# Hybrid LRU / attention / state-space backbone on one core: the state-space core starts by group and takes its steps at wider intervals

## The chip, the core and the metric

The kernel runs on one core of a Trainium2 chip, in one launch. The metric is the device time of that launch in microseconds, a median over runs. The engines are named as in the profile: PE is TensorE's matmul stream, PEld its weight loads, DVE is VectorE, ACT is ScalarE, POOL is GpSimd, SP is SyncE, which issues the transfers.

## What is computed

Two layers of a hybrid backbone over 256 context and 256 latent tokens of width 2048, in float32. Cut to what matters here:

```python
for l in range(2):
    shift, scale, gate = split(silu(cond) @ ada_w + ada_b)        # for the latents and for the context
    u = rmsnorm(x) * (1 + scale) + shift
    lx, lg, q, k, v, ag, xbc, z, dt = split_cols(u @ w_in)
    lru = rglru_mixer(lx)                                         # scan in both directions
    att = window_attention(q, k, v)                               # 8 heads, softmax over window, context and a sink
    ssd = ssd_mixer(xbc, z, dt)                                   # the state-space core, both directions
    x = x + gate * (concat(lru*silu(lg), att*silu(ag), ssd) @ w_out)

def ssd_chunked(x, dt, A, B, C, h0):                              # chunks of 128 tokens, 2 groups of 8 heads
    decay = exp(segment sums of dt * A);  W = (C . B) * decay * dt
    y_diag = W @ x                                                # inside a chunk
    states = B^T @ (x * exp(A_last - Acs) * dt);  h = exp(A_last) * h + states
    y_off = (C @ h) * exp(Acs)                                    # from the chunks before
```

`ssd_mixer` runs this twice, forwards and on the flipped sequence, and adds both. It needs xs, B and C (parts of xbc after a convolution and a silu) and dt. A group of 8 heads needs its own column of B and of C, its own four columns of xs, and dt.

## The kernel before

Weights are stored as blocks of 128x128. Every weight is split into hi (rounded to the matmul's fast float32 form, on ACT, L237) and lo (the rest, on DVE, L238), as is every activation u; a block then takes three matmuls, `hi*uh`, `hi*ul`, `lo*uh` (`mm3`, L174 is the matmul of the helper `mm`). One hi and one lo instruction serve four blocks, and there are three buffers of each (`HB`). A **tile of columns** is 128 columns of w_in: 16 blocks, 48 matmuls, of 512 token columns or, in layer 1 for what only latents need, of 256.

A layer first runs through the columns of w_in: first B, C and the first of x side by side (`HEAD`), in layer 0 with four more x between them (`FILL`), then the rest of x, then lx and lg by turns (8 each), then 8 z, 2 k, 2 v, and q and ag by turns (8 each: one attention head for every pair). Then comes w_out in three parts (`OUT_PARTS`): the LRU's eight rows, the state-space's, the attention's; 16 accumulators a part, each of 8 blocks.

What follows from a finished tile runs as a generator (`consume`): it emits instructions, yields a wait, and emits the next ones. A wait is a number of us of a modelled clock, which `mm` moves on for every matmul emitted (`WAIT`, one number per layer), or a condition. `pump` runs what is due between two blocks of the stream; `drain(until)` is called where the stream can't go on: it moves the clock to the next due time and runs the waiting generators in the order of those times until the condition holds. PE's order is the order in which the program emits; the other engines' orders come from a scheduler that places their instructions by its own estimate. All queues are in order: on PE a matmul that waits holds up all behind it.

- `ssd_core` (L612) waits until the 13 inputs (2 B, 2 C, 8 x, dt) are there. Then, for each of two groups, it makes steps: `State` (L1105: a product with Xtok on DVE, a matmul, a decayed sum on DVE) and `Output` (L1131: two decay rows by DMA, then eight DVE and eight ACT instructions over 128x128, exponentials, POOL products, and 8 to 24 small matmuls). Layer 0 has 28 steps (12 states, 16 outputs), layer 1 has 20 (12 and 8). A step's `begin` is emitted, then the core waits `WAIT["core"]` (4 us in layer 0, 5.2 in layer 1), then the step before gets its `end`, which holds its matmuls.
- `ada_wide` (L361) forms the modulation vectors that the start of a layer doesn't need, from ada_w by rows, on DVE (L380): 64 steps a part, one DMA of 256 KB into one of three buffers each. Layer 0 runs parts 0 to 2 of it after its core (that is, layer 0's gate and layer 1's shift and scale). Layer 1 runs the last one, layer 1's gate: from the head of the layer on (`ada1`, every 2.75 us), it stops when the core may begin, and goes on after the core (`ada`, every 5.97 us).
- The attention of a head (`att_q`, L802) emits scores, softmax (DVE maxima, ACT exponentials, POOL scaling, L864), then after a wait (`q2`, for the last head `q2z`: 12.98 us in layer 1) the transposes of the probabilities (L170), their split (ACT L875, DVE L877), and the product with v.
- Before the first block of w_out the layer calls `drain` until the gate vector is there:

```python
            self.drain(lambda: part in self.parts_done)
            if pi == 0:
                self.drain(lambda: self.ada_done >= (4 if l else 1))
```

The residual update of x (L1073) multiplies each accumulator of w_out by that gate; there are three accumulators (`acc`).

Of the kernel before, what the change touches and what calls it, by code (L numbers as in the profile page):

```python
# [18 lines left out]
C = 256  # L19
# [94 lines left out]
for _tag, _bufs, _roles in [  # L114
# [13 lines left out]
    for _r in _roles:  # L128
# [2 lines left out]

HB = 3
WAIT = {"B": (36.48, 14.89), "C": (28.19, 0.27), "x": (33.09, 10.71), "dt": (16.92, 0.59), "softplus":
        (19.41, 30.37), "acs": (0.94, 0.68), "core": (4, 5.2), "ada": (2.38, 5.97), "ada1": (1.17, 2.75), "z":
# [5 lines left out]
class Kernel:  # L140
# [220 lines left out]
    def ada_wide(self, parts):  # L361


        nc = self.nc
        for w in parts:
            l, part = (0, 2) if w == 0 else (1, w - 1)
            conds = 1 if w == 3 else 2
            if w < 3:
                yield lambda: self.core_done
            sums = self.t([P, conds, KT, 4], "wst" if w < 3 else "adas", 1)  # L370
            for q in range(4):
                row = [self.t([P, 4, P], "adac") for _ in range(conds)]
                for c in range(conds):
                    nc.sync.dma_start(out=row[c], in_=self.condD[4 * q:4 * q + 4, c].partition_broadcast(P))
                for m in range(KT):
                    raw = self.t([P, 512], "araw", 3)
                    nc.sync.dma_start(out=raw, in_=self.a["adaw"][w, q, m])
                    for c in range(conds):
                        o = raw if c == conds - 1 else self.ada_acc()
                        i = nc.vector.scalar_tensor_tensor(out=o, in0=raw, scalar=1.0,  # L380
                                                           in1=row[c].rearrange("p t x -> p (t x)"), op0=ALU.mult,
                                                           op1=ALU.mult, accum_out=sums[:, c, m, q:q + 1])
                        self.tc.keep_in_program_order(i)
                    yield self.wait("ada" if self.core_done else "ada1")
                    if self.ssd_ready == 13 and not self.core_done:
                        yield lambda: self.core_done
            mod = self.mods[l][:, KT * part:KT * part + KT]
            o = PARAMS["ada_b"][0] + KT * part
            for c in range(conds):
                nc.vector.tensor_reduce(out=mod[:, :, c], in_=sums[:, c], axis=AX.X, op=ALU.add)  # L390
                nc.vector.tensor_tensor(out=mod[:, :, c], in0=mod[:, :, c], in1=self.prms[l][:, o:o + KT], op=ALU.add)
            self.ada_done += 1
# [105 lines left out]
    def ssd_in(self, l, kind, i, px, t0):  # L498
        nc = self.nc
        if kind == "B":  # L500
            self.ssd_conv(8 + i, px, self.BT[:, i], 0)
            yield self.wait("B")
            self.tok_major(self.BT[:, i], self.Btok[:, :, i * P:(i + 1) * P])
        elif kind == "C":
            self.ssd_conv(10 + i, px, self.CT[:, i, t0:], t0)
            yield self.wait("C")
        else:
            xs = self.t([P, 512], "xs")
            self.ssd_conv(i, px, xs, 0)
            s = C if l else 0  # L510
            nc.gpsimd.tensor_scalar(out=self.Y[:, i, s:], in0=xs[:, s:], scalar1=self.par("Drep", i), scalar2=1.0,  # L511
                                    op0=ALU.mult, op1=ALU.mult)
            yield self.wait("x")
            self.tok_major(xs, self.Xtok[:, :, i * P:(i + 1) * P])
        self.ssd_ready += 1

    def dt_weights(self, l):
        nc = self.nc
# [26 lines left out]
    def ssd_dt2(self, dts):  # L545
# [7 lines left out]
        z = self.t([P, 2, 4, 16], "dtz", 1)  # L553
# [32 lines left out]
        self.acsD = self.dram([P, P], "acsD")  # L586
        nc.sync.dma_start(out=self.acsD, in_=at)
        yield self.wait("acs")
        self.ssd_ready += 1

    def softplus(self, z, n, tag):

# [19 lines left out]
    def ssd_core(self, l):  # L612


        yield lambda: self.ssd_ready == 13
        ends = []
        for g in range(2):
            f1, r1 = self.ssd_state(0, g, 0), self.ssd_state(1, g, 1)
            steps = [f1, r1]
            if l == 0:  # L620
# [325 lines left out]
    def layer(self, l, xs):  # L946
        nc = self.nc
        self.l = l
        mod = self.mods[l]
        self.ssd_ready = self.kv_ready = 0  # L950
        self.core_done = False
        self.lru_h, self.att_o, self.parts_done, self.mixes = {}, {}, set(), {}
        t0 = lambda kind: 0 if l == 0 or kind in CTX_COLS else C
        wst = self.blocks(self.a["w_in"][l], NW)
# [35 lines left out]
        for ct, ks in head_plan(l):  # L990
            fill = ct in FILL[l]
            acc = self.mx() if fill else accs[ct][:, cols(ct)]
            for k in ks:
# [16 lines left out]
                if k == 6 and wds is None:  # L1010
                    wds = self.dt_weights(l)
                    if l == 0:
                        i = nc.sync.dma_start(out=self.cst[:, P:], in_=self.a["consts"][:, P:])
# [43 lines left out]
        for pi, part in enumerate(OUT_PARTS):  # L1057
# [3 lines left out]
            for m in range(KT):  # L1061
# [7 lines left out]
                x = xs[m // 8][:, m % 8]  # L1069
# [205 lines left out]
```

## Time and profile before

| | |
|---|---|
| median of 3 runs | 1846.21 us (1844.5 to 1850.26) |
| the profiled execution | 1850.27 us, its span 1848.5 us |
| PE, DVE, ACT, POOL busy | 1777.5, 1424.8, 959.7, 334.9 us |
| mean granted clock of TensorE | 0.988 of full speed |
| chain that ended last | PE 74%, DVE 12%, ACT 7%, issue 4%, DMA 3% |

The span is what the profiler saw between the first and the last instruction. An engine is busy while an instruction of it runs; matmuls overlap, so a busy PE can still lose time between two starts. The arrow of a row names who ended the idle time ahead of an instruction.

### The profile page before, as it was taken

The page shows a single profiled execution, that of the slowest core. Times are in us where ns is not written, and L with a number is a line of the kernel's source. Part 1 is how long each engine was busy: PE and PEld are TensorE (multiplying, and loading weights), DVE is VectorE, ACT ScalarE, POOL GpSimd, SP SyncE. Part 2 cuts the span into 40 slices and gives each one's busy share as a digit, 9 for nine tenths or more (in the row PEclk, how much of TensorE's full clock was granted, in tenths as well). Part 3 has the DMA queues.
Part 4 walks back from the last instruction along what each step waited for, and adds up shares of the span by engine and source line. Part 5 has one row for each costly group of instructions (what it writes and reads, how often), then busy time and mean ns, then how long its engine had stood idle before and what let it go on. Part 6 is the DMA issues. An engine that isn't in the chain of part 4 may idle for free.

```text
span 1848.5 us, 29534 instructions
## 1 busy us (share of the span) xinstructions
PE 1777.5 (96%) x10522; PEld 1456.0 (79%) x10522; DVE 1424.8 (77%) x3053; ACT 959.7 (52%) x1766; POOL 334.9 (18%) x271
## 2 busy tenths in 40 slices
PE   7999999999999999999999999999999999999999
PEld 4777876666778877887878887878666788999999
DVE  4447769899998888989999547776778885788765
ACT  4324577777433354555232335544687763677543
POOL 0000124434210022221000020010243330122000
PEclk9999999999999999999999999999999999999999
DMA  9982433435775645557777443464343564555656
GB/s 377 365 295 69 124 97 106 129 111 157 220 219 175 192 145 174 172 166 245 231 221 221 129 126 107 142 183 150 96 136 109 160 202 152 174 174 165 210 184 183
DMA packets 140261, 323.09 MB, mean 175 GB/s; under 512 B 14000, under 2 KB 39504, under 8 KB 139472
## 3 DMA queue, kind: packets, MB, share of 16 engines
q1 hardware_dynamic: 140112, 321.20, 55.6%
q8 instruction: 82, 1.34, 0.3%
q14 instruction: 67, 0.55, 0.1%
HBM read 310.51 MB, written 10.63 MB: 174 GB/s over the span
## 4 chain that ended last, share of the span: by engine, by line
PE 74%; DVE 12%; ACT 7%; issue 4%; DMA 3%; POOL 1%; SPq 0%; POOLq 0%; DVEq 0%; ACTq 0%
PE acc L174 57%; PE mx L174 12%; DVE lo L238 3%; PE ada L174 3%; PE mx L170 2%; DVE ee L1161 1%; DVE ada L380 1%; ACT lt L712 1%; DVE araw L380 1%; ACT hi L237 1%; DMA bc<-acsD 1%; ACT ww L1163 1%; DMA araw<-in_adaw_dram 1%; DVE lh L730 1%; ACT ee L1160 1%
## 5 line engine op out<-in xcount | busy, mean ns | idle before, releaser
L174 PE MATMUL acc<-u,hi 128*128 128x512 f32 (+1 forms) x4800 | 1284.7, 356 | 10.7 <-ACT hi L237 6.2
L174 PEld LDWEIGHTS acc<-u,hi 128*128 128x128 f32 x4800 | 840.6, 191 | 158.3 <-issue 29.0
L174 PE MATMUL acc<-u,lo 128*128 128x512 f32 (+1 forms) x2400 | 848.8, 354 | 24.8 <-DVE lo L238 24.2
L237 ACT ACTIVATE hi<-raw 128x512 fp32r<-128x512 f32 x640 | 399.3, 629 | 588.4 <-PE acc L174 459.2
L238 DVE TENSOR_TENSOR lo<-raw,hi 128x512 fp32r<-128x512 f32 x640 | 470.1, 737 | 195.7 <-ACT hi L237 186.0
L174 PEld LDWEIGHTS acc<-u,lo 128*128 128x128 f32 x2400 | 458.0, 191 | 98.9 <-DVE lo L238 39.0
L380 DVE SCALAR_TENSOR_TENSOR araw<-araw,adac 128x512 f32<-128x512 f32 x256 | 189.5, 741 | 8.6 <-DMA araw<-in_adaw_dram 5.3
L380 DVE SCALAR_TENSOR_TENSOR ada<-araw,adac 128x512 f32<-128x512 f32 x192 | 143.1, 745 | 11.2 <-DMA araw<-in_adaw_dram 6.6
L174 PE MATMUL mx<-u,hi 128*128 128x512 f32 (+1 forms) x320 | 98.8, 392 | 0.0
L1073 DVE SCALAR_TENSOR_TENSOR X<-acc,mod,X 128x256 f32<-128x256 f32 x144 | 65.0, 478 | 38.2 <-PE acc L174 38.0
L864 POOL TENSOR_SCALAR prob<-prob,qrs 128x512 f32<-128x512 f32 (+1 forms) x48 | 58.3, 1228 | 200.0 <-ACT hi L237 158.0
L427 POOL TENSOR_TENSOR ssq<-ssq,sq 128x512 f32<-128x512 f32 (+1 forms) x26 | 32.7, 1257 | 303.2 <-ACT sq L423 303.2
L1172 POOL TENSOR_TENSOR bc<-bc,CT 128x512 f32<-128x512 f32 x40 | 62.2, 1566 | 88.2 <-ACT bc L1171 49.1
L511 POOL TENSOR_SCALAR X<-xs,prm 128x512 f32<-128x512 f32 (+1 forms) x16 | 15.4, 963 | 344.5 <-DVE xs L489 340.6
L174 PEld LDWEIGHTS mx<-u,hi 128*128 128x128 f32 x320 | 55.9, 188 | 14.1 <-issue 4.0
L720 POOL TENSOR_TENSOR la<-lt 128x512 f32<-128x512 f32 x32 | 39.0, 1221 | 134.5 <-ACT lt L718 117.1
L174 PE MATMUL mx<-u,lo 128*128 128x512 f32 (+1 forms) x160 | 60.7, 379 | 0.0
L1161 DVE SCALAR_TENSOR_TENSOR ee<-bc,nacs,ee 128x128 f32<-128x128 f32 x96 | 44.2, 509 | 18.7 <-DMA bc<-acsD 14.3
L767 POOL TENSOR_TENSOR qw<-qw,cst 128x256 f32<-128x256 f32 x20 | 22.5, 1127 | 195.2 <-DVE rt L766 131.5
L727 POOL TENSOR_TENSOR lt<-lt,ltl 128x512 f32<-128x512 f32 x32 | 47.8, 1515 | 48.4 <-ACT ltl L724 45.5
L712 ACT ACTIVATE lt<-mx,gbh 128x512 f32<-128x512 f32 x64 | 42.4, 674 | 10.0 <-PE mx L174 10.0
L174 PE MATMUL mx<-xc,gw 64*64 64x512 f32 x128 | 39.9, 615 | 4.6 <-DVE H L1128 2.2
(236 smaller groups left out, 1979.0 us busy)
## 6 DMA issues: line engine op xcount, KB each, us to landing
raw<-in_w_in_dram SPq DMA_DIRECT2D x224, 512.0 KB, 3.7
araw<-in_adaw_dram SPq DMA_DIRECT2D x256, 256.0 KB, 3.2
raw<-in_w_out_dram SPq DMA_DIRECT2D x96, 512.0 KB, 3.8
ar<-in_ada_dram SPq DMA_DIRECT2D x84, 256.0 KB, 5.9
bc<-acsD SPq DMA_DIRECT2D x48, 256.0 KB, 4.1
ar<-in_ada_dram SPq DMA_DIRECT2D x22, 512.0 KB, 7.4
adac<-condD SPq DMA_DIRECT2D x28, 256.0 KB, 4.6
gw<-in_gates_dram SPq DMA_DIRECT2D x16, 256.0 KB, 2.9
```

The source lines that it names most:

```text
L170: self.nc.tensor.transpose(out=out, in_=lhsT, identity=rhs)
L174: self.nc.tensor.matmul(out=out, lhsT=lhsT, rhs=rhs, start=start, stop=stop, **kw)
L237: nc.scalar.activation(out=hi, in_=part, func=AF.Copy)
L238: nc.vector.tensor_tensor(out=lo, in0=part, in1=hi.bitcast(F32), op=ALU.subtract)
L380: i = nc.vector.scalar_tensor_tensor(out=o, in0=raw, scalar=1.0, in1=row[c].rearrange("p t x -> p (t x)"), op0=ALU.mult, op1=ALU.mult, acc ...
L712: nc.scalar.activation(out=t, in_=pg[g], func=AF.Tanh, scale=0.5, bias=self.gb[:, 16 * g + 8 * d + m:16 * g + 8 * d + m + 1])
L720: nc.gpsimd.tensor_tensor(out=a2, in0=tr, in1=tr, op=ALU.mult)
L727: nc.gpsimd.tensor_tensor(out=ti, in0=ti, in1=tl[:, d], op=ALU.mult)
L864: nc.gpsimd.tensor_scalar(out=pr[j], in0=pr[j], scalar1=rs[:, j:j + 1], scalar2=1.0, op0=ALU.mult, op1=ALU.mult)
L1073: nc.vector.scalar_tensor_tensor(out=x[:, s], in0=acc[:, s.start - w0:s.stop - w0], scalar=mod[:, 2 * KT + m, c:c + 1], in1=x[:, s], op0=A ...
L1161: nc.vector.scalar_tensor_tensor(out=e[:, j], in0=bcs[1][:, j], scalar=k.nacs[:, r:r + 1], in1=e[:, j], op0=ALU.add, op1=ALU.min)
L1172: nc.gpsimd.tensor_tensor(out=bc, in0=bc, in1=k.CT[:, g, None, tok].to_broadcast([P, 4, P]), op=ALU.mult)
```

## The change

The count of inputs becomes a set; each group waits for its own seven inputs (B, C, four x, dt) instead of all 13; the waits between steps go from 4 and 5.2 us of the modelled clock to 5.4 and 7.6; `ada_wide` of layer 1 stops when the core has begun.

```diff
-        (19.41, 30.37), "acs": (0.94, 0.68), "core": (4, 5.2), "ada": (2.38, 5.97), "ada1": (1.17, 2.75), "z":
+        (19.41, 30.37), "acs": (0.94, 0.68), "core": (5.4, 7.6), "ada": (2.38, 5.97), "ada1": (1.17, 2.75), "z":
@@ ada_wide
                     yield self.wait("ada" if self.core_done else "ada1")
-                    if self.ssd_ready == 13 and not self.core_done:
+                    if self.core_begun and not self.core_done:
                         yield lambda: self.core_done
@@ ssd_in
-        self.ssd_ready += 1
+        self.ssd_ready.add((kind, i))
@@ ssd_dt2
-        self.ssd_ready += 1
+        self.ssd_ready.add(("dt", 0))
@@ ssd_core
-        yield lambda: self.ssd_ready == 13
         ends = []
         for g in range(2):
+            need = {("B", g), ("C", g), ("dt", 0)} | {("x", 4 * g + i) for i in range(4)}
+            yield lambda: need <= self.ssd_ready
+            self.core_begun = True
             f1, r1 = self.ssd_state(0, g, 0), self.ssd_state(1, g, 1)
@@ layer
-        self.ssd_ready = self.kv_ready = 0
-        self.core_done = False
+        self.ssd_ready, self.kv_ready = set(), 0
+        self.core_begun = self.core_done = False
```

No instruction of PE is added or removed; 8788 rows of its order stand in other places. Counted in tiles of 48 matmuls of the stream, from the first matmul with weights: in layer 0 the core's first matmul moves from tile 15.62 to 13.75 and its last group from 26.38 to 27.62 (z begins at 28); in layer 1 from 94.56 to 90.50 and from 106.81 to 107.81 (z begins at 108). So 28 steps stand on 13.9 tiles instead of 10.8, and 20 on 17.3 instead of 12.3.

**PE, layer 0, the first state of the core** (`xw` is Xtok weighted, `Btok` and `CT`, `BT` are B and C; `acc` rows are the stream, u by hi and lo). Before:

```order
L174 MATMUL acc_2595<-u_1072,hi_2634 128x512
L174 MATMUL acc_2595<-u_1073,hi_2634 128x512
L174 MATMUL acc_2595<-u_1072,lo_2635 128x512
L174 MATMUL mx_2644<-xw_2567,Btok_1769 128x512
L174 MATMUL mx_2648<-CT_1768,BT_1767 128x128
L174 MATMUL acc_2595<-u_1287,hi_2634 128x512
```

With the change:

```order
L174 MATMUL acc_2388<-u_1299,hi_2427 128x512
L174 MATMUL acc_2388<-u_1298,lo_2428 128x512
L174 MATMUL mx_2443<-xw_2351,Btok_1769 128x512
L174 MATMUL mx_2447<-CT_1768,BT_1767 128x128
L170 MATMUL mx_2479<-cst_76,xs_2151 128x128 x4
L174 MATMUL acc_2388<-u_1501,hi_2485 128x512
```

The state now stands ahead of the transposes of x's last tiles (`xs`), two tiles of the stream earlier.

**PE, layer 1, the last head's probabilities** (`prob`; `vh`, `vl` are v, `ptlh`, `ptll` the split probabilities). Before, amid w_out, whose matmuls stand on both sides:

```order
L174 MATMUL acc_17124<-u_16801,hi_17127 128x256
L174 MATMUL acc_17124<-u_16802,hi_17127 128x256
L174 MATMUL acc_17124<-u_16801,lo_17128 128x256
L170 MATMUL mx_17134<-cst_76,prob_16931 128x128 x4
L174 MATMUL acc_17124<-u_16810,hi_17127 128x256
L174 MATMUL acc_17124<-u_16811,hi_17127 128x256
```

With the change, behind the product of head 6 (`mx_16925`) and ahead of the whole of w_out:

```order
L174 MATMUL mx_16925<-ptlh_16634,vh_14693 128x256
L174 MATMUL mx_16925<-ptll_16636,vh_14693 128x256
L174 MATMUL mx_16925<-ptlh_16634,vl_14694 128x256
L170 MATMUL mx_16948<-cst_76,prob_16893 128x128 x4
L170 MATMUL mx_16956<-cst_76,prob_16895 128x128 x4
L174 MATMUL mx_16967<-ptlh_16899,vh_14693 128x256
L174 MATMUL mx_16967<-ptll_16900,vh_14693 128x256
```

Between the last scores of head 7 and these transposes now stand 4 transposes, 6 stream matmuls and the 12 of head 6's product; before there stood over 100 stream matmuls. The first w_out matmul follows the 12 of head 7's product.

**DVE, layer 1, the end of `ada_wide`** (`araw` a row of ada_w, `adas` its sums, `mod` the modulation vectors, X the residual). Before, the last steps stand amid the q tiles:

```order
L238 TENSOR_TENSOR lo_16589<-raw_16555,hi_16588 128x512
L380 SCALAR_TENSOR_TENSOR araw_16601,adas_11169<-araw_16601,adac_15138 128x512
L238 TENSOR_TENSOR lo_16610<-raw_16607,hi_16609 128x512
L390 TENSOR_REDUCE mod_33_146<-adas_11169 128x16
L766 TENSOR_TENSOR rt_3493_16579<-qw_16550,cst_76 64x256 x2
L391 TENSOR_TENSOR mod_33_146<-mod_33_146,prm_991 128x16
```

With the change they stand behind head 7's split, right ahead of the first residual updates:

```order
L380 SCALAR_TENSOR_TENSOR araw_17002,adas_11169<-araw_17002,adac_16500 128x512
L238 TENSOR_TENSOR lo_17141<-raw_17122,hi_17140 128x512
L380 SCALAR_TENSOR_TENSOR araw_17005,adas_11169<-araw_17005,adac_16500 128x512
L238 TENSOR_TENSOR lo_17161<-raw_17158,hi_17160 128x512
L380 SCALAR_TENSOR_TENSOR araw_17008,adas_11169<-araw_17008,adac_16500 128x512
L390 TENSOR_REDUCE mod_33_146<-adas_11169 128x16
L391 TENSOR_TENSOR mod_33_146<-mod_33_146,prm_991 128x16
L1075 SCALAR_TENSOR_TENSOR X_16921<-acc_17013,mod_33_146,X_16921 128x256
```

Before the core, layer 1 now has 19 of its 64 `ada_wide` steps in place of 32. Ten of them stand behind head 7's split, with six lo rows among them.

## Rows read from the trace of the kernel before

**Rows 1.** Cores of both layers: length; busy PE, PEld, DVE, ACT, POOL; clock; DMA share, GB/s.

```profile
255.00:455.00 200.00, 183.14 (x996) 128.72 (x995) 178.88 (x324) 149.04 (x296) 81.41 (x56) 0.99 0.40 114
1315.00:1465.00 150.00, 137.54 (x823) 101.93 (x822) 122.33 (x209) 111.93 (x201) 57.07 (x45) 0.97 0.41 124
```

**Rows 2.** PE's groups of instructions in layer 0's core, 255 to 455 us.

```profile
L174 PE MATMUL acc<-u,hi 128*128 128x512 f32 x360 | 118.5, 410 | 1.7 <-ACT hi L237 1.7
L174 PE MATMUL acc<-u,lo 128*128 128x512 f32 x180 | 71.5, 397 | 10.7 <-DVE lo L238 10.7
L174 PE MATMUL mx<-bc,H 128*64 128x128 f32 x192 | 19.0, 273 | 0.0
L174 PE MATMUL mx<-ee,X 128*64 128x128 f32 x128 | 18.0, 288 | 0.1
L174 PE MATMUL mx<-xc,gw 64*64 64x512 f32 x48 | 16.3, 614 | 4.3 <-DVE H L1128 2.2 <-ACT lt L712 2.0
L174 PE MATMUL mx<-xw,Btok 128*128 128x512 f32 x24 | 13.0, 626 | 0.0
```

**Rows 3.** Undisturbed pace, from the chain: start us, us, matmuls of 512 and 256 columns.

```profile
249.02 9.57 PE acc L174 x42
...
1722.67 122.06 PE acc L174 x1017
```

**Rows 4.** PE's timeline in layer 0's core: a state, gates, an output.

```profile
258.43 1.02 PE L174 MATMUL mx<-xw,Btok 128*128 128x512 f32 x2
259.28 0.38 PE L174 MATMUL mx<-CT,BT 128*128 128x128 f32 x2
...
265.25 0.65 PE L174 MATMUL mx<-xc,gw 64*64 64x512 f32 x2
...
266.27 0.73 PE L174 MATMUL acc<-u,hi 128*128 128x512 f32 x2
...
271.32 0.45 PE L174 MATMUL mx<-ee,X 128*64 128x128 f32 x4
...
272.39 0.49 PE L174 MATMUL mx<-CT,BT 128*128 128x128 f32 x2
```

**Rows 5.** DVE's groups in layer 0's core, 255 to 455 us.

```profile
L238 DVE TENSOR_TENSOR lo<-raw,hi 128x512 fp32r<-128x512 f32 x46 | 38.1, 831 | 4.3 <-ACT hi L237 4.3
L1161 DVE SCALAR_TENSOR_TENSOR ee<-bc,nacs,ee 128x128 f32<-128x128 f32 x56 | 30.6, 593 | 5.5 <-ACT ee L1160 3.0 <-DMA bc<-acsD 2.5
L1164 DVE SCALAR_TENSOR_TENSOR ww<-cbm,dt,ww 128x128 f32<-128x128 f32 x64 | 19.6, 359 | 3.3 <-ACT ww L1163 3.3
```

**Rows 6.** Layer 1's attention, heads 6 and 7: last scores (PE), scaled probabilities (POOL).

```profile
1684.32 0.39 PE L174 MATMUL mx<-kh,ql 128*128 128x512 f32 x1
...
1691.12 2.32 POOL L864 TENSOR_SCALAR prob<-prob,qrs 128x512 f32<-128x512 f32 x2 [8.56 <-ACT hi L237]
...
1699.88 0.40 PE L174 MATMUL mx<-kh,ql 128*128 128x512 f32 x1
...
1710.94 2.56 POOL L864 TENSOR_SCALAR prob<-prob,qrs 128x512 f32<-128x512 f32 x2 [13.87 <-DVE qrs L858]
```

**Rows 7.** Head 7's second split, ACT and DVE, from the timeline.

```profile
1718.42 0.60 ACT L875 ACTIVATE ptlh<-mx 128x512 fp32r<-128x512 f32 x1 [0.28 <-PE mx L170]
...
1719.05 0.76 DVE L877 TENSOR_TENSOR ptll<-mx,ptlh 128x256 fp32r<-128x256 f32 x2 [0.19 <-ACT ptlh L875]
```

**Rows 8.** The page: the costliest groups, and the transfers of ada_w's rows.

```profile
L238 DVE TENSOR_TENSOR lo<-raw,hi 128x512 fp32r<-128x512 f32 x640 | 470.1, 737 | 195.7 <-ACT hi L237 186.0
L380 DVE SCALAR_TENSOR_TENSOR araw<-araw,adac 128x512 f32<-128x512 f32 x256 | 189.5, 741 | 8.6 <-DMA araw<-in_adaw_dram 5.3
...
araw<-in_adaw_dram SPq DMA_DIRECT2D x256, 256.0 KB, 3.2
```

**Rows 9.** A wait of PE in its timeline, and the stage right after it.

```profile
363.90 0.50 PE L174 MATMUL acc<-u,lo 128*128 128x512 f32 x1 [2.60 <-DVE lo L238]
...
364.00:368.00 4.00, 4.00 (x10) 2.59 (x11) 3.10 (x7) 3.23 (x7) 1.28 (x1) 0.64 0.10 37
```

## The prediction

> **What bounds the kernel now.** Begin with the busy times of the page: PE is busy for most of the span, so what can be won is what PE loses between its matmuls. Then go to the stages in which the change moves work, the state-space cores [rows 1]. In layer 0 the stretch is 200 us, PE is idle in 200 - 183.1 = 16.9 of it and its clock stood at 0.99; VectorE is busy 178.9, that is 89%. In layer 1 it is 12.5 of 150 us, with the clock at 0.97 (4.5 us of full speed lost) and VectorE at 82%. The groups say who is late: in layer 0, 10.7 us of PE's idle time end with a `lo` of VectorE [rows 2]. VectorE's queue holds the core's instructions in one row with the splits of the weights, and when a run of the former stands ahead of a `lo`, the stream stops.
>
> Idle time is not all of the loss. The Trainium skill (Trainium Kernel Development and Optimization, Best Practices) says not to judge a kernel's distance to its limit by matmul busy time; going by busy time the core of layer 0 has 16.9 us to give, and the trace agrees with the warning, as the next count shows. Count starts instead: 42 matmuls of 512 columns take 9.57 us undisturbed, 0.228 each, and 1017 of 256 columns 122.06, 0.12 each [rows 3]. A state takes 259.28 - 258.43 = 0.85, the gates of one direction 266.27 - 265.25 = 1.02, an output 272.39 - 271.32 = 1.07 for 16 small matmuls, 0.067 each [rows 4]. Layer 0's stretch holds 540 stream matmuls (123.1 us), 320 small ones (21.4), 12 directions of gates, four of the 48 in each (12.2), and 12 states, two records each (10.2) [rows 2]. That makes 167 of 200 us: **33 us lost**, 1.7 times idle and clock together (18.9). For layer 1 the same factor on 12.5 + 4.5 = 17 gives an estimate of 29.
>
> **The change, part by part.**
>
> *Layer 0's core at wider steps.* The same steps stand on 13.9 tiles instead of 10.8. Two kinds of VectorE instructions of the outputs alone take 30.6 + 19.6 = 50.2 us [rows 5]; 22% of that, 11 us, leave the crowded stretch for tiles 13.75 to 15.6 and 26.4 to 27.6, where no step of the core stood. The core's products, states and decays go with them; I take 13 us off VectorE there, and since VectorE's lateness is what PE waits for, 13 off the 33. Bounds: nothing, if runs as long as before still stand ahead of single `lo`, and 24 if the loss falls to that of a quiet stretch. I stay below half, because VectorE is busy 178.9 us where PE's own work is 167: spreading brings the two level and leaves no large reserve.
>
> *Layer 1's core.* 20 steps on 17.3 tiles instead of 12.3, the first of them in the wide x tiles, where a `lo` is due every 12 x 0.228 = 2.7 us and not, as in the narrow tiles, every 12 x 0.12 = 1.4 [rows 3]. By the share of layer 0, 13 of 33, its 29 give 12; bounds 0 and 22.
>
> *Starting by group* costs nothing of itself: inputs are already there, and what the core's decay rows load goes on a SyncE queue that loses the ada_w rows of that time to the core's pause.
>
> *The pause of `ada_wide`.* This one has a price. It stops four tiles earlier in layer 1, with 19 of its 64 steps done in place of 32. Afterwards it runs at its old interval, so it is 13 steps late. Before, it ended amid the q tiles; now steps are left when w_out must begin, and `drain` moves the clock past them and past everything that is due before. The last head's wait (12.98 us of that clock) goes with them, so its transposes come up on PE at once (second place in the order above). How long they wait there: head 6's scores end at 1684.7 and POOL has scaled its probabilities at 1693.4, 8.7 us later; for head 7 it is 1700.3 to 1713.5, 13.2 us, as splits of the mix stand between on ACT [rows 6]. In between PE now has 4 transposes, 6 stream matmuls and 12 of head 6's product, about 0.35 + 0.7 + 1.4 = 2.5 us. So PE waits 6.2 to 10.7 us. Behind the transposes ACT and VectorE split, 1719.81 - 1718.42 = 1.4 us [rows 7], which the stream used to cover as well. Together 7.6 to 12.1; I take 11, near head 7's own, since the same splits still stand in ACT's queue.
>
> Next late is the gate. VectorE does ten steps of 0.74 [rows 8] plus six `lo` of 0.74 [rows 8] behind head 7's split, some 12 us, and some 1 us more for the sums and the first residual update. PE meanwhile has head 7's product (1.4) and three accumulators of 24 matmuls each (8.6), then it needs one back: 3 us of waiting. Ten rows through three buffers, each 3.2 us on its way [rows 8], could make that 8; a queue with slack could make it 0. I take 5. After a wait of 2.6 us the granted clock was 0.64 for four us, 1.4 lost [rows 9]; two waits cost 3 (1.5 to 4). The tail costs **11 + 5 + 3 = 19 us**, between 9 and 24.
>
> **Sum.** -13 - 12 + 19 = -6 us. The profiled execution took 1850.3, 4.1 above the median of the runs, so 1844.3 against itself and **1840** against the median of 1846.2. A measurement of this kernel tells about 0.3%, 5.5 us, from no change.
>
> **The rivals.**
>
> *VectorE stays the bound, slower.* The spread takes no instruction off VectorE. `lo` takes 831 ns in the core of layer 0 and 737 over the run [rows 5, 8], with POOL busy 81 of 200 us there [rows 1]; the spread takes nothing off POOL either. If clusters remain, the two cores give back only 9 and the tail costs 21: 1846 + 12 = 1858. It decides as soon as the cores give less than 13.5. For it: 178.9 against 167 above. Against it: the new stretches at both ends had room. The Trainium skill (GPSIMD Engine Reference, 1. Specifications) states that POOL shares its SBUF interfaces with VectorE and contends with instructions of two SBUF inputs; by that rule the extra 94 ns per `lo` move along with the core, and it speaks for this rival. The rows fit it without proving it.
>
> *Gain and tail cancel.* Cores give 19, tail 19: 1846. Nothing in the rows rules out such a pair.
>
> *The tail is short, faster.* If the scheduler's rows let head 7 go as fast as head 6 and no accumulator is waited for, the tail costs 9 and the cores give 28: 1827. Against it: the splits of the mix that delayed head 7 before stand ahead of its exponentials in ACT's queue as they did.
>
> **How the numbers follow.** Forecast 0.33 (its own range 1833 to 1843), cancelling 0.27, slower 0.23, short tail 0.17. The forecast and the short tail are faster, 0.50; the cancelling is the same, 0.27; 0.23 slower. The range takes the forecast, the cancelling and most of both outer cases, with their bounds: 1827 to 1858.
>
> **What would show it.** Right: over 255 to 455 us PE's idle time falls from 16.9 to about 10, over layer 1's core from 12.5 to about 7; PE waits for POOL's `prob` in layer 1 some 8 us in one piece, then for a residual update some 5, with the clock at half behind each. The first group's matmuls come ahead of x's last transposes. Wrong: no long wait on `prob` at the end of layer 1's w_in (then the tail is cheap), or as many waits on `lo` as before in the cores (then the spread bought nothing). If both cores gain and the tail is as said, but the time doesn't fall, look for new waits where the steps went, above all in the x tiles of layer 1.

## The result: slower, and the profile after

The changed kernel takes **1876.4 us** (median of 4 runs, 1875.6 to 1877.86) against 1846.27 before, a ratio of 1.0158 with a 95% interval of 1.0142 to 1.0175. That is 1.6% slower, and no run of one kernel comes near a run of the other (1844.5 to 1850.26 before). The forecast was 1840, in a range of 1827 to 1858. The busy times from the page of the kernel after:

```profile
PE 1786.0 (95%) x10522; PEld 1462.0 (78%) x10522; DVE 1426.4 (76%) x3053; ACT 960.6 (51%) x1766; POOL 333.7 (18%) x271
```

The instructions are the same and VectorE is as busy as before; only the order moved. The stretches that answer to [rows 1], with the same columns:

```profile
255.00:455.00 200.00, 177.62 (x914) 126.67 (x912) 157.64 (x263) 132.64 (x251) 73.50 (x52) 0.95 0.33 104
1315.00:1465.00 150.00, 138.64 (x811) 105.47 (x810) 124.03 (x191) 116.88 (x200) 60.56 (x48) 0.97 0.38 115
```

In layer 0 VectorE's busy time fell from 178.9 to 157.6 us, as a spread should make it; both windows hold the same 540 matmuls of the stream. PE's idle time rose nevertheless, from 16.9 to 200 - 177.6 = 22.4, and the clock fell from 0.99 to 0.95. PE's groups there [rows 2]:

```profile
L174 PE MATMUL acc<-u,hi 128*128 128x512 f32 x360 | 121.9, 421 | 7.2 <-ACT hi L237 7.2
L174 PE MATMUL acc<-u,lo 128*128 128x512 f32 x180 | 74.5, 414 | 12.3 <-DVE lo L238 12.2
```

PE waits for `lo` 12.2 us in place of 10.7, and for `hi` 7.2 in place of 1.7.

To see where the time went, count the stream's matmuls in the two traces (48 a tile of columns, the same work in the same order) and compare the times at which a tile starts. Five stretches, in us, for all kernels of this study, each from one trace; the last column is the ratio of all runs to runs of the kernel before made beside them, with its interval:

| kernel | tiles 13-20 | 20-36 | 36-86 | 86-135 | 135-159 | ratio of times |
|---|---|---|---|---|---|---|
| before | 108.2 | 232.4 | 628.6 | 496.8 | 146.4 | 1 |
| the change | 119.4 | 234.4 | 627.3 | 492.5 | 166.1 | 1.0158 [1.0142, 1.0175] |
| e1 layer 1 alone | 108.2 | 234.4 | 632.0 | 492.1 | 166.0 | 1.0098 [1.0082, 1.0115] |
| e2 layer 0 alone | 122.7 | 234.4 | 627.3 | 494.9 | 147.0 | 1.0085 [1.0066, 1.0103] |
| e3 pause as before | 122.6 | 234.1 | 627.7 | 496.5 | 147.5 | 1.0084 [1.0069, 1.0099] |
| e4 early, old steps | 122.8 | 227.0 | 627.3 | 507.4 | 146.4 | 1.0081 [1.0057, 1.0105] |
| e5 offset 2.8 | 108.3 | 235.7 | 624.0 | 494.5 | 146.2 | 0.9988 [0.9973, 1.0003] |
| e6 late, wide steps | 103.9 | 250.2 | 624.0 | 495.7 | 146.6 | 1.0049 [1.0032, 1.0066] |
| e7 step 4.2 | 108.3 | 235.1 | 625.3 | 494.8 | 146.4 | 0.9988 [0.9976, 1.0000] |
| e8 layer 1, mended | 108.2 | 233.5 | 627.8 | 494.7 | 149.8 | 1.0005 [0.9995, 1.0016] |
| e9 offset 1.4 | 111.5 | 224.6 | 624.6 | 495.2 | 146.8 | 0.9956 [0.9941, 0.9971] |
| e10 old steps, offset | 114.1 | 233.0 | 624.8 | 497.8 | 146.8 | 1.0012 [1.0001, 1.0022] |
| e11 both offset | 108.3 | 233.9 | 625.7 | 499.6 | 147.6 | 1.0033 [1.0023, 1.0044] |
| e12 change, mended | 111.8 | 224.8 | 625.3 | 492.5 | 149.8 | 0.9963 [0.9950, 0.9975] |

Layer 0's core lies in tiles 13 to 28 (the second column runs on to 36, since the variants end their core at different places), layer 1's in 90 to 108, the last heads and the start of w_out in 135 to 159. So the change lost 11.2 + 2.0 us around layer 0's core, won 4.3 around layer 1's and lost 19.7 at the end.

One trace of a stretch isn't exact. The change, e2 and e3 have the same order of PE, DVE, ACT and POOL up to tile 36 and take 119.4, 122.7 and 122.6 us in tiles 13 to 20. The kernel before and e1 share theirs too: 108.2 both times, but 232.4 and 234.4 in tiles 20 to 36, so the 2.0 there is no more than spread. Layer 0's loss is 11 to 14.5 us, all of it in tiles 13 to 20.

The 4.3 us of layer 1 don't lie in the core's own tiles. Tiles 90 to 108 and 108 to 120, before, with the columns of [rows 1]:

```profile
1243.40:1471.70 228.30, 213.91 (x1216) 164.44 (x1217) 176.83 (x297) 155.64 (x271) 71.55 (x57) 0.96 0.42 127
1471.70:1577.90 106.20, 101.12 (x643) 89.94 (x642) 72.07 (x130) 54.89 (x94) 21.41 (x20) 0.98 0.57 173
```

and after:

```profile
1254.10:1483.00 228.90, 213.75 (x1218) 163.76 (x1217) 173.14 (x274) 157.49 (x272) 71.85 (x59) 0.97 0.36 112
1483.00:1585.60 102.60, 99.82 (x642) 88.46 (x641) 69.73 (x127) 52.78 (x91) 22.28 (x20) 1.00 0.59 186
```

The core's tiles take 228.3 and 228.9 us. The tiles behind it take 106.2 and 102.6, and PE's idle time there falls from 5.1 to 2.8 us.

Layer 0's first stretch, before:

```profile
226.40:334.60 108.20, 103.62 (x532) 74.13 (x531) 85.70 (x148) 78.74 (x150) 39.49 (x28) 1.00 0.39 112
```

and after:

```profile
226.10:345.50 119.40, 107.52 (x549) 77.76 (x548) 96.01 (x164) 83.57 (x162) 43.95 (x30) 0.96 0.33 106
```

Idle time goes from 4.6 to 11.9 us, 7.3 of the 11.2. The other 3.9 are busy time: two steps more stand in the stretch (13 in place of 11), about 1 us of PE each by the prediction's counts, and the rest is what the clock, at 0.96, costs while PE works. What stops PE there is to be seen in VectorE's timeline after the change. Between two `lo` stands one block of other work:

```profile
248.24 1.11 DVE L238 TENSOR_TENSOR lo<-raw,hi 128x512 fp32r<-128x512 f32 x1 [0.46 <-ACT hi L237]
249.27 0.68 DVE L723 SCALAR_TENSOR_TENSOR ltl<-la,ltl 128x512 f32<-128x512 f32 x1
250.43 0.42 DVE L1189 TENSOR_TENSOR X<-mx,X 128x256 f32<-128x256 f32 x1 [0.48 <-PE mx L174]
250.85 0.49 DVE L1149 TENSOR_TENSOR cbm<-mx,cst 128x128 f32<-128x128 f32 x2
252.04 3.03 DVE L1163 SCALAR_TENSOR_TENSOR ee<-bc,nacs,ee 128x128 f32<-128x128 f32 x4 [0.71 <-ACT ee L1162]
255.00 1.21 DVE L732 TENSOR_TENSOR_SCAN lh<-lt,lt 128x512 f32<-128x512 f32 x1
256.14 1.11 DVE L1166 SCALAR_TENSOR_TENSOR ww<-cbm,dt,ww 128x128 f32<-128x128 f32 x4
257.17 0.68 DVE L735 TENSOR_TENSOR_SCAN lh<-lt,lt 128x256 f32<-128x256 f32 x1
257.77 2.15 DVE L1166 SCALAR_TENSOR_TENSOR ww<-cbm,dt,ww 128x128 f32<-128x128 f32 x4
259.84 0.74 DVE L737 TENSOR_TENSOR_SCAN lh<-lt,lh,lt 128x256 f32<-128x256 f32 x1
260.50 0.66 DVE L1117 TENSOR_TENSOR xw<-X,wst 128x512 f32<-128x512 f32 x1
261.09 0.68 DVE L238 TENSOR_TENSOR lo<-raw,hi 128x512 fp32r<-128x512 f32 x1
```

From 249.3 to 261.1 no `lo` comes: the core's `cbm`, `ee`, `ww` and `xw` and the LRU's scans add up to 11.2 busy us. A weight buffer lasts PE 12 x 0.228 = 2.7 us [rows 3] and there are three, 8.2 us. The longest such blocks in this stretch add up to 6.8 and 6.4 us before, 11.2 and 10.5 after. PE's answer, at this block and at the second one:

```profile
261.82 0.50 PE L174 MATMUL acc<-u,lo 128*128 128x512 f32 x1 [2.41 <-DVE lo L238]
...
333.34 0.73 PE L174 MATMUL acc<-u,hi 128*128 128x512 f32 x2 [3.84 <-ACT hi L237]
336.38 0.79 PE L174 MATMUL acc<-u,lo 128*128 128x512 f32 x1 [2.31 <-DVE lo L238]
```

The stages around the second, with the clock in the third column from the right:

```profile
333.00:337.00 4.00, 1.35 (x4) 0.82 (x5) 4.00 (x9) 3.00 (x6) 2.60 (x2) 0.63 0.00 0
337.00:341.00 4.00, 4.00 (x11) 3.13 (x10) 2.88 (x4) 1.57 (x3) 0.47 (x1) 0.51 0.36 135
```

PE waits 3.84 and 2.31 us, and then runs at half clock for four more with work at hand. The wait for `hi` has the same origin: ACT's `ww`, ahead of it in ACT's queue, waits 5.87 us for VectorE's `cbm`, which stands in that block:

```profile
328.78 1.57 ACT L1165 ACTIVATE ww<-cbm,dt 128x128 f32<-128x128 f32 x5 [5.87 <-DVE cbm L1149]
```

The end, in layer 1:

```profile
1719.65 1.97 PE L170 MATMUL mx<-cst,prob 128*128 128x128 f32 x8 [6.83 <-POOL prob L866]
1722.30 0.58 PE L174 MATMUL mx<-ptlh,vh 128*128 128x256 f32 x1 [0.69 <-ACT ptlh L877]
1740.41 0.76 PE L174 MATMUL acc<-u,hi 128*128 128x256 f32 x2 [5.45 <-DVE X L1075]
```

and VectorE just ahead of the last row: the gate's last sum, then the residual update that PE waits for.

```profile
1739.57 0.17 DVE L391 TENSOR_TENSOR mod<-mod,prm 128x16 f32<-128x16 f32 x1
1739.78 1.27 DVE L1075 SCALAR_TENSOR_TENSOR X<-acc,mod,X 128x256 f32<-128x256 f32 x3
```

Two stages of this end, behind the first wait and around the second; the clock is at 0.50 and 0.53:

```profile
1722.00:1726.00 4.00, 3.70 (x16) 3.52 (x17) 1.68 (x6) 0.63 (x2) 0.00 (x0) 0.50 0.53 164
1740.00:1744.00 4.00, 3.59 (x17) 3.62 (x18) 1.25 (x4) 0.63 (x1) 0.00 (x0) 0.53 0.01 4
```

### The profile page after: what moved, and what is told of

It reads as the page before. It is cut to its first block, busy times and chain, and to the rows that moved or that the text cites. A ratio compares the mean times of both kernels' runs of the same rounds, so it can differ in the third digit from the quotient of the medians.

```text
span 1875.0 us, 29540 instructions
## 1 busy us (share of the span) xinstructions
PE 1786.0 (95%) x10522; PEld 1462.0 (78%) x10522; DVE 1426.4 (76%) x3053; ACT 960.6 (51%) x1766; POOL 333.7 (18%) x271
## 4 chain that ended last, share of the span: by engine, by line
PE 75%; DVE 12%; ACT 5%; issue 3%; DMA 3%; POOL 1%; SPq 0%; POOLq 0%; DVEq 0%; ACTq 0%
PE acc L174 57%; PE mx L174 14%; DVE lo L238 3%; PE ada L174 2%; PE mx L170 2%; DMA araw<-in_adaw_dram 1%; DMA bc<-acsD 1%; DVE araw L380 1%; DVE ee L1163 1%; DVE ada L380 1%; ACT lt L714 1%; POOL prob L866 1%; DVE lh L732 1%; ACT hi L237 1%; DVE ww L1166 1%
## 5 line engine op out<-in xcount | busy, mean ns | idle before, releaser
L380 DVE SCALAR_TENSOR_TENSOR araw<-araw,adac 128x512 f32<-128x512 f32 x256 | 184.7, 723 | 12.6 <-DMA araw<-in_adaw_dram 6.7
L380 DVE SCALAR_TENSOR_TENSOR ada<-araw,adac 128x512 f32<-128x512 f32 x192 | 142.4, 742 | 12.4 <-DMA araw<-in_adaw_dram 11.2
L1174 POOL TENSOR_TENSOR bc<-bc,CT 128x512 f32<-128x512 f32 x40 | 57.2, 1438 | 142.9 <-ACT bc L1173 74.8
L1163 DVE SCALAR_TENSOR_TENSOR ee<-bc,nacs,ee 128x128 f32<-128x128 f32 x96 | 43.2, 500 | 28.6 <-DMA bc<-acsD 27.1
L769 POOL TENSOR_TENSOR qw<-qw,cst 128x256 f32<-128x256 f32 x20 | 22.4, 1119 | 195.5 <-DVE rt L768 101.5
```

What stands on the lines that cost most here:

```text
L1163: nc.vector.scalar_tensor_tensor(out=e[:, j], in0=bcs[1][:, j], scalar=k.nacs[:, r:r + 1], in1=e[:, j], op0=ALU.add, op1=ALU.min)
L1174: nc.gpsimd.tensor_tensor(out=bc, in0=bc, in1=k.CT[:, g, None, tok].to_broadcast([P, 4, P]), op=ALU.mult)
```

## Experiments

### One layer at a time

Waits and start condition of one layer as before, of the other as in the change:

```diff
-"core": (5.4, 7.6)
+"core": (4, 7.6)      # e1, layer 0 waits for all 13 inputs
+"core": (5.4, 5.2)    # e2, layer 1 waits for all 13 inputs
```

> Layer 0's core as before (all 13 inputs, 4 us), layer 1 with the change. The trace of the change lays 13 us of the 30 lost on layer 0's core, so the theory that layer 0's new places cost by themselves expects 1876 - 13 = 1863 us. The rival that layer 0's loss is bound to layer 1 (one schedule for the whole program) expects 1876 still, or under 1857.

> Layer 0 with the change, layer 1's core as before (all 13 inputs, 5.2 us, ada_wide stops when they are there). If layer 0's core costs 13 us by itself: 1846 + 13 = 1859 us, with the granted clock in layer 0's core near 0.95 and no wait of PE for prob at the end of layer 1. If layer 0's places are neutral and all comes from layer 1: 1846 us.

Layer 1 alone: 1866.8 us, with the tail (166.0) and the gain ahead of it (492.1). Layer 0 alone: 1864.6, with the loss in tiles 13 to 20 (122.7) and no tail. Both losses are there by themselves, so neither needs the other layer's change. They add up to 1.83%, the change loses 1.58%; the 5 us between have the size of the spread of layer 0's stretch. Both times lie 4 to 6 us above what was expected (1863 and 1859).

### The pause as before

```diff
-                    if self.core_begun and not self.core_done:
+                    if len(self.ssd_ready) == 13 and not self.core_done:
```

> The change with one part undone: ada_wide of layer 1 stops only when all 13 inputs are there, so it has 32 steps behind it again, and head 7's probabilities stand amid w_out as before. The theory that the earlier stop alone makes the tail expects 1876 - 20 = 1856 us, no wait of over 2 us for prob and none for a residual update; the steps that now stand beside the core's first steps in layer 1 may cost some 3 us. The rival that the tail comes from the core's later end expects the wait to stay, 1876.

1863.6 us, 7 above the 1856 of the first theory. The tail is gone (147.5), so the pause made it. Layer 0's loss stays (122.6), 3 of the 7, and layer 1 has no gain left (496.5): with the rows of ada_w beside the core its tiles 90 to 108 take 232.9 us in place of 228.9.

### Early start with the old steps

The change with its old steps, and the pause as in e3:

```diff
-"core": (5.4, 7.6)
+"core": (4, 5.2)
-                    if self.core_begun and not self.core_done:
+                    if len(self.ssd_ready) == 13 and not self.core_done:
```

> Cores start by group, steps at the old waits of 4 and 5.2 us, ada_wide stops as before (no tail). Layer 0's core stands on tiles 13.5 to 24.2. If it is the wider steps that hurt layer 0, the core loses what it did before: 1846 us or a little less. If it is the early start (the steps beside x's last tiles and the transposes), it stays near 1856. If any new arrangement of the steps costs, because the old one had been fitted to its waits, it lies between or above.

1863.6 us, slower than either theory had it. Layer 0's early part holds 17 steps here instead of 11, by the prediction's counts some 6 us more work, and takes 14.6 more; tiles 20 to 36 give 5.4 back; layer 1 loses 10.6. So an early start costs by itself, 9 us in layer 0, and wider steps alone can't be what costs there. The longest block is only 7.7 us here; PE's two long waits in tiles 13 to 20 are 2.79 us for a step's `ee` and 3.02 for a `lo`.

### Moving the two halves of a step apart

In the kernel before and in the change, a step's `end` and the `begin` of the step after next are emitted at the same moment of the modelled clock. This edit ends the step before in between (layer 0 only; layer 1 as before):

```diff
-                yield self.wait("core")
+                yield 2.6 if l == 0 else self.wait("core")
                 if len(ends) > 1:
                     ends.pop(0).end()
+                if l == 0:
+                    yield 2.8
```

My theory at that point was that wide steps hold the buffers of decay rows longer, so that these rows load late.

> Layer 0's core begins by group and steps every 5.4 as in the change, but the second half of a step now follows 2.6 after the next step's first half, so a step holds its buffers for 8.0 of the clock, as before the change (4 + 4), and not for 10.8; layer 1's core as before. Theory 'held longer' (decay rows come late because buffers come free late): most of the 15.9 us that layer 0's core lost with the longer hold comes back, 1847 to 1853, and VectorE waits for decay rows some 4 us in the core as before, not 9 to 13. Theory 'early start' (the steps that now stand among the x tiles are the cost): 1859 to 1866. Theory 'fitted' (the old numbers suit each other and every other arrangement loses some): 1852 to 1866.

1846.2 us, against 1864.6 of e2, which differs in this edit alone: layer 0's loss is gone, at the same start and the same wide steps. But VectorE still waits 9.7 us for decay rows (13.5 in the change, 4.3 before), so their lateness is not what decided. The stretch from tile 13 to 20, with 12 steps in it:

```profile
226.70:334.90 108.20, 102.91 (x525) 73.95 (x523) 87.96 (x153) 80.02 (x155) 42.10 (x28) 1.00 0.36 113
```

and VectorE's timeline at the place of the block above:

```profile
249.32 1.11 DVE L239 TENSOR_TENSOR lo<-raw,hi 128x512 fp32r<-128x512 f32 x1 [0.53 <-ACT hi L238]
...
253.44 0.49 DVE L1154 TENSOR_TENSOR cbm<-mx,cst 128x128 f32<-128x128 f32 x2 [1.02 <-PE mx L175]
255.00 2.29 DVE L737 TENSOR_TENSOR_SCAN lh<-lt,lt 128x512 f32<-128x512 f32 x1 [1.07 <-POOL lt L734]
257.21 1.71 DVE L239 TENSOR_TENSOR lo<-raw,hi 128x512 fp32r<-128x512 f32 x1
...
263.79 0.68 DVE L239 TENSOR_TENSOR lo<-raw,hi 128x512 fp32r<-128x512 f32 x1
```

The same work, but a `lo` stands in the middle of it. The longest block of the stretch is 5.5 us, the clock stays at 1.00. What this kernel doesn't win, it loses ahead of tile 28: two waits are each rounded up to the next block of the stream, so the steps come later, the last two outputs come up together when z begins, and at 475 us a gate's matmul on PE waits 5.45 us for VectorE's `H`, a state.

### Wide steps without the early start, and a small change of the step

Both layers wait for all 13 inputs as before:

```diff
-"core": (4, 5.2)      # the kernel before
+"core": (5.4, 5.2)    # e6
+"core": (4.2, 5.2)    # e7
```

> Layer 0's core takes the change's steps of 5.4 but waits for all 13 inputs as before; layer 1 as before. 'Held longer': still slower, 1853 to 1862. 'Early start': no loss, 1840 to 1847, since the early start alone cost 8.5 us of it. 'Fitted': 1850 to 1862.

> Everything as before the change, but layer 0's core steps every 4.2 and not every 4.0, so its matmuls stand at tiles 15.62 to 26.56 in place of 15.62 to 26.38. 'Held longer' and 'early start': within 2 us of before, 1844 to 1849. 'Fitted': a change as small as this already loses 4 us or more, 1850 to 1860.

Wide and late: 1858.1 us, but nothing is lost in tiles 13 to 20 (103.9, with 8 steps instead of 11), though a block of 11.8 us there ends in a wait of 3.16. Four steps are left over when z begins, and all of them come up at once:

```profile
483.49 0.66 PE L175 MATMUL mx<-ee,X 128*64 128x128 f32 x2 [7.00 <-DVE ee L1172]
```

That is the loss of this run (tiles 20 to 36 take 250.2 us), so although 1858 lies in the ranges of 'held longer' and 'fitted', it says little on either. The step of 4.2: 1845.0 us, as before, so 'fitted' falls; the old numbers are no narrow optimum.

### Blocks or buffers

Another offset, where a buffer is held for 9.4 (e9), and the old start and steps with an offset, held for 5.4 (e10); layer 0 only:

```diff
-                yield 2.6 if l == 0 else self.wait("core")     # e5
+                yield 4.0 if l == 0 else self.wait("core")     # e9
+                yield 1.4 if l == 0 else self.wait("core")     # e10, all 13 inputs
                 if len(ends) > 1:
                     ends.pop(0).end()
                 if l == 0:
-                    yield 2.8     # e5
+                    yield 1.4     # e9
+                    yield 2.6     # e10
```

> As the run with the short hold (layer 0's core by group, one step per 5.4; layer 1 as before), but the second half of a step follows 4.0 after the next step's first half, so a step holds its buffers for 9.4, between 8.0 (1846 us) and 10.8 (1865 us). Theory 'held longer': the loss grows with the time a buffer is held, so this lies in the middle, 1852 to 1859. Theory 'clumps' (a step's second half and the next but one's first half fall on the same moment, so one block of VectorE work with no lo in it grows to 11 us and PE, whose three weight buffers last 8 us in the wide tiles, stops and loses its clock; any offset between the halves breaks the block): no block over 7 us in tiles 13 to 22 and the time of the short hold, 1843 to 1849.

> Layer 0's core waits for all inputs and takes one step per 4.0 as before the change, but the second half of a step follows 1.4 after the next step's first half (held 5.4 in place of 8.0; two waits in place of one are rounded up twice, so the core ends near tile 28 and not at 26.4); layer 1 as before. 'Held longer': shorter is better, 1836 to 1845. 'Clumps': the order of VectorE's instructions has a few blocks of 6 to 9 us between two lo, as before the change has, so no gain and at most a small loss, 1845 to 1855.

"Held longer" falls with e9: held 9.4, the kernel takes 1840.9 us and is faster than before. Held 5.4, it takes 1852.3, against that theory too, but for a reason of its own (below). "Clumps" gave the right side of both, with a part of its wording wrong. In e9 a block of 8.3 us is left in tiles 13 to 20, and PE waits for it; the time lies below the 1843 to 1849 expected. And in e10 the offset breaks nothing: its longest blocks are 10.6 and 10.0 us in tiles 13 to 20, not 6 to 9.

```profile
266.12 0.79 PE L175 MATMUL acc<-u,lo 128*128 128x512 f32 x1 [3.94 <-DVE lo L239]
```

That explains its 111.5 us in place of 108.2. The gain is behind it: tiles 20 to 36 take 224.6 in place of 232.4. From tile 20 to 28, 337.6 to 470.3 us, PE's waits are

```profile
PE acc L175 <- DVE lo L239: 3.9, 3, 3.0
PE acc L175 <- ACT hi L238: 2.0, 2, 1.0
PE mx L175 <- ACT lt L719: 0.4, 1, 0.4
PE mx L175 <- DVE H L1135: 0.2, 1, 0.2
```

6.5 us in place of the 12.5 that the kernel before waits in the same tiles. In e10 the waits from 225 to 490 us show a third way to lose:

```profile
PE mx L175 <- DVE ee L1174: 15.4, 5, 6.2
PE acc L175 <- DVE lo L239: 5.3, 5, 1.7
```

A step that is ended 5.4 after its begin has its products not ready, and PE waits for them instead of for `lo`.

Why does a block of 8.3 us cost 3.94 in e9? The kernel before has one of 8.7 us, from 373 to 382 us, that costs nothing. Its two neighbours of kind `lo` on VectorE's queue:

```profile
371.93 1.28 DVE L238 TENSOR_TENSOR lo<-raw,hi 128x512 fp32r<-128x512 f32 x2
...
382.15 0.68 DVE L238 TENSOR_TENSOR lo<-raw,hi 128x512 fp32r<-128x512 f32 x1
```

and those of the block in e9:

```profile
256.51 1.33 DVE L239 TENSOR_TENSOR lo<-raw,hi 128x512 fp32r<-128x512 f32 x1
...
265.39 0.68 DVE L239 TENSOR_TENSOR lo<-raw,hi 128x512 fp32r<-128x512 f32 x1
```

The traces tell how many buffers of `lo` were full when a block began: those that VectorE had ended, less what PE's matmuls had begun to use (a quarter for each block of weights). Nine gaps of over 7 us between two `lo` in layer 0's core, with no wait of PE for a gate or a step in between:

| kernel, gap between two `lo` | its length, us | buffers full at its start | PE's wait for the next `lo`, us |
|---|---|---|---|
| before, 373.2 to 382.2 | 8.9 | 2.75 | 0 |
| the change, 382.7 to 392.2 | 9.5 | 3.00 | 0 |
| e6, 400.6 to 410.0 | 9.4 | 2.75 | 0 |
| the change, 249.3 to 261.1 | 11.7 | 2.50 | 2.41 |
| the change, 326.0 to 335.2 | 9.2 | 1.00 | 2.31, after 3.84 for `hi` |
| the change, 364.8 to 373.4 | 8.6 | 1.00 | 3.08 |
| the change, 400.9 to 408.2 | 7.3 | 1.25 | 2.75 |
| e6, 451.0 to 459.7 | 8.7 | 1.00 | 4.89 |
| e9, 257.8 to 265.4 | 7.5 | 1.25 | 3.94 |

With nearly three buffers full, a gap of 9.5 us costs nothing. With 1 to 1.25, 7.3 us cost 2.75. The ten other such gaps of these four kernels, with 1.5 to 2.75 full, end in waits of 0 to 3.16. In e9 a block of 5.8 us and a single `lo` stand ahead of the 8.3 us. So the length of a block is half of the account, and how far the buffers had filled up ahead of it the other half.

### Layer 1 mended, and the whole change mended

The put-off rows of ada_w come closer together after layer 1's core, with layer 0 as before (e8), with layer 0 as in e9 (e12), and with an offset in both layers (e11):

```diff
-"ada": (2.38, 5.97)
+"ada": (2.38, 4.25)    # e8, with "core": (4, 7.6); e12, with the offset of e9
+"ada": (2.38, 4.0)     # e11
-                yield self.wait("core")
+                yield (2.6, 2.8)[l]     # e11
                 if len(ends) > 1:
                     ends.pop(0).end()
+                yield (2.8, 4.8)[l]     # e11
```

> Layer 0's core as before; layer 1's core begins by group and steps every 7.6, as in the change; the steps of the ada_w rows that the longer pause put off are caught up at an interval of 4.25 in place of 5.97, so that the last head's work stands where it stood before. If the tail's 20 us come from the put-off rows and layer 1's core gains 4 us by itself: 1842 to 1847. If the rows that now stand closer after the core cost VectorE time there: 1848 to 1854. If the tail has another cause than the rows: 1860 to 1868.

> The whole change, with three edits: second halves follow 2.6 (layer 0) and 2.8 (layer 1) after the next step's first half, at one step per 5.4 and 7.6 as in the change; and the put-off ada_w rows come every 4.0 in place of 5.97, so that the last head's products stand where they stood before the change. 'Clumps': layer 0 like the short hold (-1 against before), layer 1 gains 3 to 6 and the tail gives back up to 3: 1840 to 1847. 'Held longer': the same or a little better, 1838 to 1847. If layer 1's earlier start clumps with the x tiles in spite of the offset: 1850 to 1860.

> The whole change with two edits: in layer 0 the second half of a step follows 4.0 after the next step's first half and 1.4 ahead of the one behind it (as in the run that held 9.4), and the put-off ada_w rows come every 4.25 in place of 5.97. If the parts add: layer 0 -8 against before, layer 1 with the rows mended 0 (-2 to +2 in the run with layer 1 alone mended), so 1837 to 1844. If layer 0's gain depends on what follows it, or layer 1's earlier core clumps again: 1846 to 1856.

e8: 1847.5 us; the tail costs 3.4 in place of 19.7, and layer 1 gains 2.1, no more than spread, so nothing is left over. e11: 1854.4 us; with the offset layer 1 takes 499.6 in place of 492.5 to 494.7 without it (e12, e8), so the offset that helps in layer 0 doesn't help there, and the expected 1840 to 1847 was missed. The time lies in the range of its third case, blocks in spite of the offset, but no run tells whether that is the reason; the rows of ada_w also come closer, every 4.0. e12: 1842.8 us, inside its expectation: the parts add. The lowest of all is e9, layer 0's core early, wide and offset, layer 1 untouched: 1840.9 against 1849.0 of the kernel before beside it; its interval overlaps with that of e12.

## Why the prediction was wrong

**The tail came as described, and its sum is right in part by luck.** Forecast: 11 (6.2 to 10.7 of it the wait for `prob`, 1.4 for the split) + 5 + 3 = 19 us. Measured, 19.7 in all: a wait of 6.83 for `prob` and two for the split of 1.6 together, 8.4 in place of the 11; 5.45 for the residual update; and 5.8 for the rest, the clock at 0.50 and 0.53 and small waits, in place of the 3. The two errors cancel. e3 shows that the pause made the tail, e8 and e12 that an earlier catch-up takes most of it away.

**Layer 1's core gave nothing in its own tiles.** "By the share of layer 0, 13 of 33, its 29 give 12" gave 12; measured 4.3, and against the six other runs whose layer 1 was as before (e2, e5, e6, e7, e9, e10: 494.5 to 497.8) between 2 and 5. PE's idle time in the window fell from 12.5 to 11.4 us, not to 7. And the gain is not where the forecast had it: the core's own tiles take 228.3 and 228.9 us, and what was won lies behind them. Why the tiles behind gain was not tested. The share was carried over from a term that was itself wrong.

**Layer 0's core had the wrong sign, and that decided.** Forecast -13, measured +13.2; that is 26 of the 36 us between forecast and result, layer 1 is 8. Four sentences failed.

- "Tiles 13.75 to 15.6 and 26.4 to 27.6, where no step of the core stood" was true, but other work of VectorE stood there. In e2, e3, e4 and the change, all of which put steps there with their halves on one moment, tiles 13 to 20 take 119 to 123 us; PE stood idle for 4.6 there before. There was little to win and a quiet stretch to lose.
- "And since VectorE's lateness is what PE waits for, 13 off the 33" turned busy time into lateness. VectorE's load in the stretch did fall, by 21 us of 200, and PE waited longer. What PE waits for is not VectorE's load but the next `lo`, and the buffers that are full when a block begins cover only so much of it. e5 has the change's steps, moves only the halves apart, and the loss of this stretch is gone.
- "Bounds: nothing, if runs as long as before still stand ahead of single `lo`, and 24": the lower bound left out that the blocks could get longer, and the clock's price was charged in the tail alone. In layer 0 it went from 0.99 to 0.95 over 200 us, at most 8 us, since a part of that falls on PE's waits.
- "*Starting by group* costs nothing of itself" was put down for the inputs and the loads alone. In e4, with the old steps, the early start costs 9 us in layer 0; it needs the offset as well to come free.

The rival "VectorE stays the bound" named the right engine and the wrong effect: it let the cores give 9. None of my cases had a core that loses.

**The idea behind the forecast holds in part, where the blocks are broken.** In e9 and e12 the early start with wider steps wins 7.6 to 7.8 us in tiles 20 to 36 and loses 3.3 to 3.6 in tiles 13 to 20: 4 us by these traces, less than the 13. The median of e9's runs is 8 us below the kernel before; most of the rest lies in tiles 36 to 86 (624.6 in place of 628.6), where kernels with layer 0 as before take 627.8 to 632.0, so that part is not shown to be the steps' doing.

What stays open: why layer 1 gains behind its core and not in it, and why with an offset (e11) it loses 5 to 7 against an early core without one.

## What to carry to other kernels

Where a stream on one engine is fed by splits that share an in-order queue with other work, judge a reordering by the longest blocks of other work between two feeds, and by how many buffers are full when each begins, and not by the queue's load. Work that moves into a "free" stretch should be given an offset from what is already emitted at the same moments; here, with layer 0's core early and wide, 1.4 or 2.8 us between the two halves of a step made the difference between 1865 and 1841 to 1846 us. An offset is no cure by itself: with the old start and steps it cost 2 to 3 us (e10), and in layer 1 it didn't help (e11). When a pause is moved, look at once for where its rest of work comes up, since a forced drain pulls everything that is due.

## What the runs showed of the hardware

The clock after a wait. In the change the granted clock stood at 0.63 and 0.51 around waits of 3.84 and 2.31 us. Right behind the single wait of 2.41 us at 261.82 it shows 0.57, with PE at work all the time:

```profile
262.00:266.00 4.00, 4.00 (x11) 3.13 (x12) 4.00 (x7) 0.39 (x1) 3.92 (x3) 0.57 0.64 199
```

while the kernel before has waits of 1.72 and 2.36 us some 7 us apart and shows

```profile
280.00:300.00 20.00, 15.77 (x89) 11.83 (x88) 19.58 (x27) 13.20 (x25) 12.30 (x8) 1.00 0.31 86
```

1.00 over both. So of two waits of about 2.4 us one cost its length alone, and the other 1.7 us more (0.43 of four us); the length doesn't tell which.

VectorE beside POOL. In the block above four `ww` took 1.11 us at 256.14 and 2.15 at 257.77. The second four were not all slower: three took 0.32 to 0.34 us like the first four, and one took 1.39. That one, and POOL in the same stretch:

```profile
258.01 1.39 DVE L1166 SCALAR_TENSOR_TENSOR ww<-cbm,dt,ww 128x128 f32<-128x128 f32 x1
...
251.80 2.61 POOL L729 TENSOR_TENSOR lt<-lt,ltl 128x512 f32<-128x512 f32 x2 [3.00 <-ACT ltl L726]
257.78 1.47 POOL L1174 TENSOR_TENSOR bc<-bc,CT 128x512 f32<-128x512 f32 x1 [3.37 <-ACT bc L1173]
```

It began amid POOL's product and ended 0.15 us behind it. In the trace of the change 22 of the `ww` and `ee` (L1163) took over 0.5 us; each of them ended 0.15 us behind an instruction of POOL, and none that began while POOL was at work was short. So VectorE isn't slowed by some share there: its instruction is held until POOL's is done. The Trainium skill (GPSIMD Engine Reference, 1. Specifications) states that the two engines contend where VectorE's instruction has two SBUF inputs, as `ww` and `ee` do, and the trace agrees. In the block above three such holds, two of `ee` and one of `ww`, make an estimated 2.9 of the 11.2 us (1.20, 1.38 and 1.39 in place of 0.34 each). No run took POOL's work away to show how much of the loss that is. All kernels have such holds: over tiles 13 to 20, the time beyond the median of VectorE's instructions within which one of POOL ended adds up to 14.0 us before, 15.8 in the change, 13.1 in e5 and 18.5 in e9. So their sum alone doesn't tell the kernels with the loss from those without.
